# Gate and up products in the order wide, wide, narrow, narrow, and a planner with a larger margin and fewer weight pieces

## The chip, the core and the metric

The kernel runs on one core of one Trainium2 chip. The metric is the device time of one execution in microseconds (us). Three timed runs of the kernel before gave 1286.79, 1289.82 and 1290.23 us; the median is 1289.82. The profiled execution is one more run with times of its own. TensorE is called PE in the rows, VectorE DVE, ScalarE ACT, GpSimd POOL and SyncE, whose queue issues the transfers here, SP.

## The reference: what is computed

Two layers of a hybrid decoder trunk run over 256 positions of width 1024, all in float32:

```python
for l in range(DEPTH):                       # 2 layers, D_FF = 2816
    x = x + 0.5 * swiglu(rms_norm(x, ffn1_norm[l]), ffn1_w_gate_up[l], ffn1_w_down[l])
    u = rms_norm(x, mix_norm[l]) @ w_in[l]
    ...                                      # u is split: SSD, mLSTM and RWKV-7 mixers
    y = jnp.concatenate([y_ssd, y_ml, y_rw], axis=-1)
    x = x + y @ w_out[l]
    x = x + 0.5 * swiglu(rms_norm(x, ffn2_norm[l]), ffn2_w_gate_up[l], ffn2_w_down[l])
return rms_norm(x, final_norm)

def swiglu(x, w_gate_up, w_down):
    gate, up = jnp.split(x @ w_gate_up, 2, axis=-1)
    return (jax.nn.silu(gate) * up) @ w_down
```

So there are four feed-forward stages (two in each layer) with a mixer stage between the two of each layer. Each layer's weights are read once.

## The kernel before

**Split products.** TensorE multiplies in a reduced float32 format. To keep float32 accuracy each operand is split into a high part (ScalarE copies it into that format, L821 for weights) and a low part (VectorE subtracts, L822), and a product is hi x hi + hi x lo + lo x hi. `mm3` (L853 to L856) does this with three matmuls.

**A gate and up block.** A feed-forward stage has 22 blocks of 128 gate and 128 up columns. The first two are computed together in another form; the other 20 are done by `gate_up`. There the activations are the moving operand: `hT.both(kk)` is the high and the low part of one 128-row slice of the normalised input side by side, 512 columns, and `hT(kk)[0]` is the high part alone, 256 columns. For each slice kk (8 of them) and each of gate and up (g) there is a wide matmul (L1073, weights' high part against both, 512 columns into the whole bank) and a narrow one (L1075, weights' low part against the high part, 256 columns into the bank's second half). A block is 16 wide and 16 narrow matmuls, into two banks. The kernel before issues wide, narrow for gate, then wide, narrow for up; for the last slice the narrow one goes first, so that the wide one (L1078) closes the bank. Behind each block come the down products of the block two before it (`down`, 12 matmuls of 512 columns, by `mm3`).

**The mixers.** The input projection `w_in` is computed in blocks of 24 matmuls of 256 columns (`block`, by `mm3`) and in wide parts. Each block's result goes through a token shift (L1185) or three convolution steps on VectorE (L1195). Beside these dense products run three chains of small dependent work: the gates (VectorE lines L1557 to L1621 with transposes L1552, L1595, L1618 and sums L1582), mLSTM and SSD (the exponentials' rows by L1631 and L1632, mLSTM's first products L1653 with its weights wq, wk, wv read by L1647), and RWKV. The RWKV chain matters below: 32 small matmuls (L1299) are masked on VectorE (L1304, eight operations), parts of the result go to memory in 32 small transfers (L1338) and come back as one tile (L1341), thirty small VectorE steps solve a triangular system in it (L1364, L1366), the result goes through memory again (L1371, L1372, L1380), and TensorE continues with transposes that are told to wait for the solve (L1388, L1398) and with the block products of L1428 and L1474.

**What sets the order.** The program is recorded, and a planner (class `Planner`) then simulates the engines with its own costs and emits the instructions in the order in which it placed them. Each engine's queue, and the queue of transfers, keeps that order on the chip. For an instruction whose inputs come from another engine the planner lets TensorE count it as due only MARGIN ns after these inputs are ready, by its own clock; a dense product that is due earlier goes first (`est`). This delay is only in the choice: no wait is put into the program. `allowed` limits how many weight pieces are held: raw ones as they land ("f") and split ones ("r"), at least wmin, at most wmax and only while enough room is left. `keep` holds room back for the mixers' tiles; the values are tried in order until a plan succeeds, which it does at 4096.

Of the kernel before, what the change touches and what calls it, by code (L numbers as in the profile page):

```python
# [28 lines left out]
T = 256  # L29
# [128 lines left out]
class Planner:  # L158


    SEM = 60.0
    MARGIN = 1000.0
    SWITCH = 1283.0

    def __init__(self, nc, pool, banks, smalls):
# [194 lines left out]
    def run(self, reserve, wmin, wmax, urgent, keep_max, spare):  # L360
# [132 lines left out]
        def est(op):  # L493
# [7 lines left out]
            if op.eng == "pe" and op.cross > 0:  # L501
                t = max(t, op.cross + self.MARGIN)
            if op.lock:
# [124 lines left out]
def kernel(ctx: ExitStack, tc: tile.TileContext, x, pvec, prow, fnorm, w_gate,  # L628
# [28 lines left out]
    banks = [psum.tile([128, 512], F32, name=f"bank{i}") for i in range(8)]  # L657

    plan = Planner(nc, ctx.enter_context(tc.tile_pool(name="regions", bufs=1)), banks, smalls)
    pe, act, dve, gps, sp = (plan.engine(n) for n in ("pe", "act", "dve", "gps", "sp"))  # L660
# [347 lines left out]
    def ffn(inp, update, make_next, first=None):  # L1008
# [3 lines left out]
        hT = inp.hT  # L1012
# [47 lines left out]
        def gate_up(j, R):  # L1060


            banks = [mmb(), mmb()]
            for i in range(2):
                (w,) = weights(1)
                wh, wl = (v.rearrange("p (k g c) -> p k g c", k=4, g=2) for v in w[1:])
                with dense(w):
                    for k in range(4):
                        kk = 4 * i + k
                        for g in range(2):  # L1070
                            o = banks[g]
                            if kk < 7:
                                pe.matmul(o, lhsT=wh[:, k, g, :], rhs=hT.both(kk), start=kk == 0, stop=False,  # L1073
                                          skip_group_check=True)
                            pe.matmul(o[:, T:], lhsT=wl[:, k, g, :], rhs=hT(kk)[0], start=False, stop=False,  # L1075
                                      skip_group_check=True)
                            if kk == 7:
                                pe.matmul(o, lhsT=wh[:, k, g, :], rhs=hT.both(kk), start=False, stop=True,  # L1078
                                          skip_group_check=True)
            with ranked(1):  # L1080
                s, u = new(T), new(T)
                hi, lo = pt_pair(j, 1)
# [832 lines left out]
    for l in range(DEPTH):  # L1915
# [2 lines left out]
        inp, update = ffn(inp, update, lambda: ToFfn(pv[:, l + 1, C_N1:C_N1 + 8]) if l + 1 < DEPTH  # L1918
                          else ToOut(fnorm[0:D]))
    inp.tile(1, update)  # L1920
    assert any(plan.run(reserve={"f": 6144, "r": 6144}, wmin={"f": 4, "r": 4}, wmax={"f": 5, "r": 6},
                        urgent={"act": 7000.0, "dve": 5500.0}, keep_max=keep, spare=8)
               for keep in (3072, 4096, 6144, 8192)), plan.jam
    with tc.manual_schedule():
        plan.emit()
    return plan
# [58 lines left out]
```

## Time and profile before

| what | value |
|---|---|
| median of three runs | 1289.82 us |
| profiled execution, its own time | 1287.25 us |
| its span, first to last instruction | 1285.5 us |
| TensorE busy | 1248.3 us, 97% of the span |
| VectorE, ScalarE, GpSimd busy | 70%, 55%, 7% |
| read from memory | 207 MB, 162 GB/s over the span |

The stages by the time in the span: feed-forward to about 195 us, the first mixer to about 450, two feed-forward stages to about 830, the second mixer to about 1085, the last feed-forward stage. In a row of a table by stage stand the window, its length, busy time of PE, weight loads, DVE, ACT and POOL with their counts, then the granted TensorE clock, the DMA share and GB/s. A row in order of time has start, duration, engine, line, operation, output and input, size, count, and in brackets the idle time before it and what ended it. Matmuls overlap, so their pace is the distance of their starts. A row of waits has the total, the number and the longest, in us.

### The profile page before, as it was taken

What the parts mean: (1) busy time and instruction counts of PE and PEld (TensorE: products, weight loads), DVE (VectorE), ACT (ScalarE), POOL (GpSimd) and SP (SyncE); (2) the same over time, 40 slices, a digit from 0 to 9 for tenths busy, and PEclk for the clock granted to TensorE, in tenths of its full rate; (3) what the DMA queues carried; (4) which work ended last, traced back from release to release, by engine and by line L of the source; (5) the groups of instructions that cost most, each with busy time, mean ns of one, the idle gap of its engine ahead of it and who ended that gap; (6) DMA issues with size and microseconds to landing.
All of it is one profiled execution on the core that took longest, in us unless ns stands there. A gap on an engine that the chain in (4) does not pass through costs nothing.

```text
span 1285.5 us, 20959 instructions
## 1 busy us (share of the span) xinstructions
PE 1248.3 (97%) x7938; PEld 1074.8 (84%) x7938; DVE 897.2 (70%) x1448; ACT 713.0 (55%) x1237; POOL 86.3 (7%) x153
## 2 busy tenths in 40 slices
PE   8999999998999999999999999999899999999997
PEld 6888887987997888888888888789889888888886
DVE  7766666984798476666676666669837993766664
ACT  7555546665655365555565555565557553655553
POOL 3000002110100010000000000111100110000001
PEclk9999999999999999999999999999999999999999
DMA  9986663042168486665575764630513576757500
GB/s 304 362 279 187 184 179 83 1 131 42 52 198 278 147 287 206 196 196 145 164 215 169 218 186 135 164 97 3 141 33 116 177 260 202 214 180 210 167 1 33
DMA packets 281876, 210.22 MB, mean 164 GB/s; under 512 B 23856, under 2 KB 257200, under 8 KB 281776
## 3 DMA queue, kind: packets, MB, share of 16 engines
q1 hardware_dynamic: 281776, 208.89, 53.3%
q8 instruction: 62, 1.02, 0.3%
q14 instruction: 38, 0.31, 0.1%
HBM read 207.01 MB, written 1.84 MB: 162 GB/s over the span
## 4 chain that ended last, share of the span: by engine, by line
PE 85%; DVE 7%; ACT 4%; issue 1%; SPq 1%; DMA 1%; POOL 0%; POOLq 0%; DVEq 0%; ACTq 0%
PE bank L1073 20%; PE bank L855 13%; PE bank L854 13%; PE bank L856 13%; PE bank L1075 12%; PE bank L1078 3%; PE bank L1428 2%; DVE region L822 1%; PE bank L1805 1%; DVE region L1195 1%; ACT region L821 1%; PE bank L1492 1%; PE bank L1511 1%; ACT region L886 1%; PE bank L1662 1%
## 5 line engine op out<-in xcount | busy, mean ns | idle before, releaser
L822 DVE TENSOR_TENSOR region<-region,region 128x1024 fp32r<-128x1024 f32 (+1 forms) x382 | 444.3, 1208 | 52.7 <-ACT region L821 49.8
L1073 PE MATMUL bank<-region,region 128*128 128x512 f32 x1120 | 398.2, 398 | 0.0
L854 PE MATMUL bank<-region,region 128*128 128x512 f32 (+1 forms) x1104 | 387.6, 351 | 0.8 <-DVE region L1304 0.4
L856 PE MATMUL bank<-region,region 128*128 128x512 f32 (+1 forms) x1104 | 385.8, 350 | 0.3 <-DVE region L873 0.3
L855 PE MATMUL bank<-region,region 128*128 128x512 f32 (+1 forms) x1104 | 385.9, 350 | 0.0
L821 ACT ACTIVATE region<-region 128x1024 fp32r<-128x1024 f32 (+1 forms) x382 | 376.7, 1038 | 12.0 <-PE bank L855 4.8
L1075 PE MATMUL bank<-region,region 128*128 128x256 f32 x1280 | 346.5, 281 | 0.0
L1073 PEld LDWEIGHTS bank<-region,region 128*128 128x128 f32 x1120 | 210.4, 188 | 50.9
L1075 PEld LDWEIGHTS bank<-region,region 128*128 128x128 f32 x1280 | 241.6, 189 | 6.6
L855 PEld LDWEIGHTS bank<-region,region 128*128 128x128 f32 x1104 | 211.5, 192 | 27.9 <-issue 2.0
L856 PEld LDWEIGHTS bank<-region,region 128*128 128x128 f32 x1104 | 211.3, 191 | 27.7 <-issue 1.7
L854 PEld LDWEIGHTS bank<-region,region 128*128 128x128 f32 x1104 | 211.4, 191 | 25.9 <-DVE region L1304 0.8
L1086 ACT ACTIVATE region<-bank 128x256 f32<-128x256 f32 (+1 forms) x84 | 30.9, 373 | 220.1 <-PE bank L1078 220.1
L1088 DVE TENSOR_TENSOR region<-bank,region 128x256 f32<-128x256 f32 (+1 forms) x84 | 34.2, 411 | 126.8 <-ACT region L1086 126.8
L873 DVE TENSOR_TENSOR region<-region,region 128x256 fp32r<-128x256 f32 (+2 forms) x88 | 37.0, 425 | 35.6 <-ACT region L872 35.6
L1090 ACT ACTIVATE region<-region 128x256 f32<-128x256 f32 (+1 forms) x84 | 34.0, 408 | 49.2 <-DVE region L1089 49.2
L1078 PE MATMUL bank<-region,region 128*128 128x512 f32 x160 | 60.2, 399 | 0.0
L872 ACT ACTIVATE region<-region 128x256 fp32r<-128x256 f32 (+2 forms) x88 | 36.2, 416 | 37.6 <-DVE region L1092 37.3
L886 ACT ACTIVATE region<-res 128x512 f32<-128x512 f32 x28 | 17.6, 628 | 56.2 <-DVE res L882 53.8
L890 POOL TENSOR_SCALAR smalls<-smalls 128x1 f32<-128x1 f32 x14 | 6.7, 476 | 617.7 <-ACT region L886 617.5
L1195 DVE SCALAR_TENSOR_TENSOR region<-bank,pv,region 128x255 f32<-128x255 f32 (+2 forms) x84 | 39.9, 479 | 7.2 <-ACT region L1193 5.3
L1092 DVE TENSOR_TENSOR region<-region 128x256 f32<-128x256 f32 (+1 forms) x75 | 31.6, 422 | 11.4 <-ACT region L1090 4.2
(304 smaller groups left out, 1075.5 us busy)
## 6 DMA issues: line engine op xcount, KB each, us to landing
region<-in_f_gu_dram SPq DMA_DIRECT2D x352, 256.0 KB, 4.8
region<-in_f_dn_dram SPq DMA_DIRECT2D x88, 512.0 KB, 4.8
region<-in_w_in_dram SPq DMA_DIRECT2D x80, 512.0 KB, 4.5
region<-in_w_out_dram SPq DMA_DIRECT2D x32, 512.0 KB, 4.8
region<-in_prow_dram SPq DMA_DIRECT2D x4, 512.0 KB, 5.1
region<-in_prow_dram SPq DMA_DIRECT2D x6, 256.0 KB, 3.9
region<-in_w_gate_dram SPq DMA_DIRECT2D x2, 512.0 KB, 4.8
dn<-region SPq DMA_DIRECT2D x64, 4.0 KB, 1.4
```

What stands on the lines that cost most here:

```text
L821: act.activation(out=hi[:, c], in_=src[:, c], func=AF.Copy)
L822: dve.tensor_tensor(out=lo[:, c], in0=src[:, c], in1=hi[:, c].bitcast(F32), op=ALU.subtract)
L854: pe.matmul(o, lhsT=ah, rhs=bh, start=start, stop=False, skip_group_check=True)
L855: pe.matmul(o, lhsT=ah, rhs=bl, start=False, stop=False, skip_group_check=True)
L856: pe.matmul(o, lhsT=al, rhs=bh, start=False, stop=stop, skip_group_check=True)
L872: act.activation(out=hi, in_=src, func=AF.Copy)
L873: dve.tensor_tensor(out=lo, in0=src, in1=hi.bitcast(F32), op=ALU.subtract)
L1073: pe.matmul(o, lhsT=wh[:, k, g, :], rhs=hT.both(kk), start=kk == 0, stop=False, skip_group_check=True)
L1075: pe.matmul(o[:, T:], lhsT=wl[:, k, g, :], rhs=hT(kk)[0], start=False, stop=False, skip_group_check=True)
L1078: pe.matmul(o, lhsT=wh[:, k, g, :], rhs=hT.both(kk), start=False, stop=True, skip_group_check=True)
L1088: dve.tensor_tensor(out=s[:, ts], in0=gate[:, ts], in1=s[:, ts], op=ALU.add)
L1195: dve.scalar_tensor_tensor(out=dst[:, s:T], in0=ps[:, 0:T - s], scalar=col(cw + 3 - s), in1=dst[:, s:T], op0=ALU.mult, op1=ALU.add)
```

## The change

Three edits. `gate_up` issues, for each slice, the two wide products and then the two narrow ones; the last slice is treated like the others, so that a narrow product closes each bank. MARGIN goes from 1000 to 2000 ns. The planner may hold 4 raw and 5 split weight pieces in place of 5 and 6, and its list of `keep` values begins at 4096.

```diff
     SEM = 60.0
-    MARGIN = 1000.0
+    MARGIN = 2000.0
     SWITCH = 1283.0
...
                     for k in range(4):
-                        kk = 4 * i + k
                         for g in range(2):
-                            o = banks[g]
-                            if kk < 7:
-                                pe.matmul(o, lhsT=wh[:, k, g, :], rhs=hT.both(kk), start=kk == 0, stop=False,
-                                          skip_group_check=True)
-                            pe.matmul(o[:, T:], lhsT=wl[:, k, g, :], rhs=hT(kk)[0], start=False, stop=False,
-                                      skip_group_check=True)
-                            if kk == 7:
-                                pe.matmul(o, lhsT=wh[:, k, g, :], rhs=hT.both(kk), start=False, stop=True,
-                                          skip_group_check=True)
+                            pe.matmul(banks[g], lhsT=wh[:, k, g, :], rhs=hT.both(4 * i + k), start=i == k == 0,
+                                      stop=False, skip_group_check=True)
+                        for g in range(2):
+                            pe.matmul(banks[g][:, T:], lhsT=wl[:, k, g, :], rhs=hT(4 * i + k)[0], start=False,
+                                      stop=i == 1 and k == 3, skip_group_check=True)
...
-    assert any(plan.run(reserve={"f": 6144, "r": 6144}, wmin={"f": 4, "r": 4}, wmax={"f": 5, "r": 6},
+    assert any(plan.run(reserve={"f": 6144, "r": 6144}, wmin={"f": 4, "r": 4}, wmax={"f": 4, "r": 5},
                         urgent={"act": 7000.0, "dve": 5500.0}, keep_max=keep, spare=8)
-               for keep in (3072, 4096, 6144, 8192)), plan.jam
+               for keep in (4096, 6144, 8192)), plan.jam
```

Since five lines go, the lines below `gate_up` are five lower in the changed kernel (L1304 becomes L1299, L1338 becomes L1333, L1398 becomes L1393, L1653 becomes L1648), and the wide and narrow products are L1070 and L1073.

On TensorE, at the start of a gate and up block of the first feed-forward stage (bank4 and bank5 are gate and up; the regions are split weights and activations), before the change:

```order
L856 MATMUL bank2_89<-region4_276,region9_235 128x512
L1073 MATMUL bank4_91<-region2_129,region6_628 128x512
L1075 MATMUL bank4_91<-region2_129,region6_628 128x256
L1073 MATMUL bank5_92<-region2_129,region6_628 128x512
L1075 MATMUL bank5_92<-region2_129,region6_628 128x256
```

and after it, where bank2 and bank3 are gate and up:

```order
L856 MATMUL bank5_92<-region6_152,region10_239 128x512
L1070 MATMUL bank2_89<-region4_134,region7_366 128x512
L1070 MATMUL bank3_90<-region4_134,region7_366 128x512
L1073 MATMUL bank2_89<-region4_134,region7_366 128x256
L1073 MATMUL bank3_90<-region4_134,region7_366 128x256
```

The second wide product now follows a wide one, and the two narrow ones stand together.

On VectorE, in the first layer's mixer, around the eight masked products (region_2180 is the first half of the RWKV matrix; region_1040 holds the gates), before:

```order
L1289 TENSOR_TENSOR region_1841<-region_2120,region_911 128x1024
L822 TENSOR_TENSOR region_352<-region_584,region_352 128x1024
L822 TENSOR_TENSOR region_498<-region_1040,region_498 128x1024
L822 TENSOR_TENSOR region_1753<-region_584,region_1753 128x1024
L1304 TENSOR_TENSOR region_2180<-bank_88,maskar 128x4x128
...
L1304 TENSOR_TENSOR region_347<-bank_88,maskar 128x4x128
L1557 TENSOR_TENSOR region_1040<-bank_89,sgn 128x72
L1561 SCALAR_TENSOR_TENSOR region_1040<-region_1040 128x72
```

and after (region_2192 and region_298 are the matrix's halves, region_752 the gates):

```order
L1284 TENSOR_TENSOR region_1096<-region_2135,region_2035 128x1024
L1552 TENSOR_TENSOR region_752<-bank_87,sgn 128x72
...
L822 TENSOR_TENSOR region_134<-region_1096,region_134 128x1024
L1561 TENSOR_TENSOR region_752<-region_752 128x72
...
L1567 SCALAR_TENSOR_TENSOR region_752<-region_752 128x72
L1299 TENSOR_TENSOR region_2192<-bank_90,maskar 128x4x128
L1299 TENSOR_TENSOR region_2192<-bank_91,maskar 128x4x128
L1567 SCALAR_TENSOR_TENSOR region_752<-region_752 128x72 x3
L1299 TENSOR_TENSOR region_2192<-bank_92,maskar 128x4x128
...
L1567 SCALAR_TENSOR_TENSOR region_752<-region_752 128x72 x2
```

The gates' steps moved ahead of the masks, and six of the eight masks stand behind four of the gates' steps.

On the queue of transfers, behind the 32 small ones to `dn` of the same layer (weight blocks of `w_in` by L746), before:

```order
L1338 DMA dn<-region_347 16x4x16
L746 DMA region_2420<-in_w_in_dram 128x8x128 x2
L746 DMA region_781<-in_w_in_dram 128x8x128
L1647 DMA region_454<-in_wq_dram 128x4x128
L1341 DMA region_1040<-dn 128x256
L1647 DMA region_454<-in_wk_dram 128x4x128
L1647 DMA region_454<-in_wv_dram 128x4x128
```

and after:

```order
L1333 DMA dn<-region_298 16x4x16
L1642 DMA region_2431<-in_wq_dram 128x4x128
L1642 DMA region_2431<-in_wk_dram 128x4x128
L1642 DMA region_2431<-in_wv_dram 128x4x128
L746 DMA region_2453<-in_w_in_dram 128x8x128
L1336 DMA region_1954<-dn 128x256
```

The three weights of mLSTM come directly behind the small transfers, and a weight block stands ahead of the read back. Ahead of the first small transfer stood 92 pieces of weights, and now 89 do.

## The prediction

> **What bounds the kernel now.** I read the page's engine totals first, then busy time by stage, then TensorE's rows in order of time, and last who waits for whom in the mixers.
>
> ```profile
> span 1285.5 us, 20959 instructions
> PE 1248.3 (97%) x7938; PEld 1074.8 (84%) x7938; DVE 897.2 (70%) x1448; ACT 713.0 (55%) x1237; POOL 86.3 (7%) x153
> ...
> 500.00:550.00 50.00, 50.00 (x264) 42.73 (x264) 33.19 (x48) 26.22 (x43) 0.00 (x0) 1.00 0.62 189
> ...
> 245.00:295.00 50.00, 44.36 (x369) 42.12 (x368) 43.47 (x107) 26.60 (x59) 9.48 (x18) 0.95 0.33 91
> 295.00:345.00 50.00, 47.84 (x701) 43.84 (x699) 26.24 (x55) 31.07 (x70) 3.09 (x4) 0.98 0.14 28
> ...
> 830.00:880.00 50.00, 47.27 (x294) 41.29 (x293) 37.11 (x46) 30.73 (x49) 7.61 (x11) 0.93 0.30 83
> 880.00:930.00 50.00, 44.28 (x374) 41.31 (x372) 44.30 (x105) 28.64 (x63) 9.19 (x18) 0.99 0.32 90
> 930.00:980.00 50.00, 48.72 (x703) 44.88 (x702) 22.01 (x39) 31.13 (x67) 1.86 (x2) 0.98 0.17 35
> ```
>
> TensorE (PE) is the bound. In the feed-forward stages (500 to 550) it is never idle, so there only the matmuls' own pace counts. In the mixers it is idle for 5.6 of 50 us in the first layer's middle and 5.7 in the second's, and its granted clock falls: 1 minus the clock times the window gives 2.5 + 1.0 us in the first layer and 3.5 + 0.5 + 1.0 in the second, 8.5 us of lost pulses. These are two separate accounts, and the change touches each with a different part.
>
> **The order of gate and up products.** A busy figure for a pipelined matmul is not its pace, so I take start times.
>
> ```profile
> 110.05 0.28 PE L1075 MATMUL bank<-region,region 128*128 128x256 f32 x1
> ...
> 111.47 0.28 PE L1075 MATMUL bank<-region,region 128*128 128x256 f32 x1
> ...
> 111.81 0.40 PE L1075 MATMUL bank<-region,region 128*128 128x256 f32 x2
> 112.05 0.40 PE L1078 MATMUL bank<-region,region 128*128 128x512 f32 x1
> ...
> 112.87 0.40 PE L855 MATMUL bank<-region,region 128*128 128x512 f32 x1
> ...
> 115.37 0.39 PE L1073 MATMUL bank<-region,region 128*128 128x512 f32 x1
> ```
>
> From 110.05 to 111.47 lie four pairs of a wide (512 columns) and a narrow (256) product: 1.42 / 4 = 0.355 us each. From 112.87 to 115.37 lie eleven wide products behind one another (the down products): 2.50 / 11 = 0.227. The two narrow ones that already stand together take 112.05 - 111.81 = 0.24, or 0.12 each. So a pair costs 0.008 us more (0.355 against 0.227 + 0.120) than its parts cost next to their own kind: a wide product pays about 8 ns when a narrow one stood before it. Today 15 of a block's 16 wide products follow a narrow one. In the new order 7 do, and the block now ends narrow, so that the first down product becomes an eighth. Seven turns fewer x 8 ns x 80 blocks (20 in each of four feed-forward stages) = 4.5 us. Against it: a narrow product alone between two wide ones takes 0.11 to 0.12, so that the second narrow of a pair may cost up to 4 ns more; 7 more such pairs x 4 ns x 80 = 2.2 us. I take the middle, -3.3 us, between 0 (the pace depends on the sum of columns alone) and -4.5. No stage hides it, since TensorE has no idle time there. What the block leaves behind: the gate bank used to be complete one narrow and one wide product before the block's end and is now complete one narrow product before it, 0.23 us later. Its evacuation feeds a down product two blocks on, over 8 us later, so this costs nothing outside the last block of a stage.
>
> **Weights held.** The planner keeps one raw and one split piece less, and TensorE's weights are converted less far ahead. In the feed-forward stages the conversions have room: VectorE (DVE) is busy 33 of 50 us. I cost this at 0; what hides it is the pieces still held, and if that cover were gone a piece would be late by the conversion (the L822 row below), about 1.2 us each time. The list of reserves without 3072 changes nothing: the plan is made with 4096 in both kernels.
>
> **The margin.** It delays TensorE's dependent matmuls by 1 us against the planner's own clock and lets dense products stand in front of them. It can win only where TensorE now waits:
>
> ```profile
> PE bank L1398 <- DVE region L1621: 2.4, 1, 2.4
> ...
> PE bank L1428 <- issue: 1.0, 2, 0.5
> ...
> PE bank L1582 <- DVE region L1578: 1.0, 1, 1.0
> PE bank L1299 <- DVE region L1304: 0.9, 1, 0.9
> PE bank L1474 <- ACT region L1399: 0.9, 1, 0.9
> PE bank L1631 <- DVE region L1366: 0.6, 1, 0.6
> ...
> PE bank L1398 <- DVE region L1195: 2.3, 1, 2.3
> ...
> PE bank L1582 <- DVE region L1185: 1.4, 1, 1.4
> ...
> PE bank L1428 <- issue: 0.9, 1, 0.9
> ...
> PE bank L922 <- ACT region L926: 0.7, 2, 0.3
> ```
>
> The first six rows are layer 0's (the L1299 wait is in both layers), the next three layer 1's, the last one the start of a feed-forward stage. Without L1299, which waits for a bank and not for the margin, layer 0 has 5.9 us and layer 1 has 4.6. The three later feed-forward starts may lose a third of 0.7 each: -0.7 us.
>
> In the mixers the new order does not only push matmuls back; it also changes what the RWKV chain waits for on VectorE and on the DMA queue (SP).
>
> ```profile
> 256.28 4.87 DVE L1304 TENSOR_TENSOR region<-bank,maskar 128x512 f32<-128x512 f32 x8
> ...
> 258.19 15.85 SPq L1338 DMA_DIRECT2D dn<-region  x32
> ...
> 277.91 0.58 SPq L1341 DMA_DIRECT2D region<-dn  x1
> ...
> 279.01 0.51 SPq L1647 DMA_DIRECT2D region<-in_wv_dram  x1
> ...
> 291.34 0.17 DVE L1366 TENSOR_TENSOR region<-region 128x15 f32<-128x15 f32 x1
> ...
> 293.56 0.98 PE L1398 MATMUL bank<-ident,region 128*128 128x128 f32 x4 [2.37 <-DVE region L1621]
> ...
> region<-in_wv_dram SPq DMA_DIRECT2D x2, 256.0 KB, 4.5
> ...
> L822 DVE TENSOR_TENSOR region<-region,region 128x1024 fp32r<-128x1024 f32 (+1 forms) x382 | 444.3, 1208 | 52.7 <-ACT region L821 49.8
> ...
> L1195 DVE SCALAR_TENSOR_TENSOR region<-bank,pv,region 128x255 f32<-128x255 f32 (+2 forms) x84 | 39.9, 479 | 7.2 <-ACT region L1193 5.3
> ```
>
> The chain: eight mask products (L1304) end at 261.1; the queue writes them out with 32 issues in 15.85 us; the read back (L1341) is at 277.9; thirty small VectorE steps (L1364, L1366) end at 291.5; then the transposes of L1398 may start, which now wait 2.4 us. In the new VectorE order the gate chain comes ahead of the masks and the last six masks stand behind four of its L1572 steps. That puts the masks about 3.5 us later (two conversions of 1.21 leave their front; the small gate steps, one conversion and the gates' detour over ScalarE come in), and with them the 32 issues, wq, wk, wv and every weight piece behind. Inside the thirty steps there now stand three conversions and six L1195 operations, where three L1195 stood: 3 x 1.21 + 3 x 0.48 = 5.0 us more. The steps started some 1.4 us after their data could be there (277.9 + 0.6 + some 3 us) because of a conversion and a triple ahead of them, which are gone: in sum 3.5 + 5.0 - 1.4 = 7.1, an estimate, so the solve ends at 298.6.
>
> TensorE, meanwhile, has 35 more narrow products ahead of L1398 (35 x 0.12 = 4.2 us), six more pairs of L1631 and L1632, and one more of L1653. By the rows below a pair takes 2 x 0.12.
>
> ```profile
> 284.63 0.28 PE L1631 MATMUL bank<-br,selr 128*128 128x256 f32 x1
> ...
> 284.98 0.28 PE L1632 MATMUL bank<-maskr,identr 128*128 128x256 f32 x1
> ```
>
> That is 4.2 + 1.4 + 0.2 = 5.8 us. It would have come to L1398 at 293.56 - 2.37 = 291.2, so now at 297.0. On the way it meets a new wait: ten pairs, which now begin near 281, stand ahead of the first L1653 products, so these are due at about 282 to 283, and wv, third behind the 32 issues, lands near 258.2 + 3.5 + 15.9 + 2 + 4.5 = 284.1: I take 2 us. The waits of L1631 (0.6) and its neighbour go. So it reaches L1398 at 297 to 298.5 and waits 0 to 1.6 more; I take 1.5, because the steps' own start is the loosest number. What is late next: the second pair of DMA trips (L1371 to L1380) starts 7 us later, but 65 more dense products stand in front of L1428, so the L1474 and L1428 waits should go. Layer 0: 1.0 (L1582) + 2 + 1.5 = 4.5 against 5.9, -1.4; layer 1, with the same order, 4.5 against 4.6, -0.1. Bounds: all of these waits gone, -10.5; the two waits at 4 and 5 us in each layer, 1.0 + 9 = 10 against 5.9 and 4.6, +9.5. The value is near the middle, since chain and cover move back by nearly the same.
>
> **Sum.** -3.3 - 0.7 - 1.5 = -5.5. The profiled execution took 1287.25 us (span 1285.5), 2.6 below the median of 1289.82; I make the sum against the former, 1281.8, and put the same distance back on for the median: 1284.3.
>
> On the order, the Trainium skill (TensorE: Matmul & The Clock Gate, section Back-to-back issue gap) gives columns / 2.4 + 2.5 ns for a matmul behind another, which does not depend on the neighbour. By it the order would be worth 0; the 0.355 against 0.347 above speaks against it, by little.
>
> **Rivals.** *The margin takes nearly all the waits* (18%): the dense products last longer than the chain is late. For it: TensorE gets 5.8 us more cover. Against: the chain moves by 7.1. Eight of the 10.5 us go, and lost pulses with them: the five windows above are idle for 17.5 us and lose 8.5, so 0.49 us for each idle one (in the forecast's 1.5 this is left out, as too little to end a low stretch). 1289.8 - 3.3 - 0.7 - 8 x 1.49 = 1273.9.
>
> *The order is worth nothing* (21%): columns alone set the pace, and 0.355 is something else, such as the change of bank. The rest stays: 1289.8 - 2.2 = 1287.6.
>
> *Slower* (17%): the queue behind the 32 issues decides. One queue holds the masks' writes, wv and the weight pieces of the next blocks; three pieces fewer stand ahead of it (89 against 92), and TensorE needs piece 89 now only 38 narrow products (4.6 us) after the first L1653. If the masks are over 5 us late, wv lands after 286 and the solve ends after 301: waits of 4 and 5 us in each layer, +9.5, with the pulses x 1.49: 1289.8 - 4.0 + 14.2 = 1300. Against it: the queue stands still for 44 us today, and no weight is late.
>
> ```profile
> SPq L1338 <- DVE region L1304: 44.3, 2, 44.0
> ```
>
> On that price, the Trainium skill (TensorE: Matmul & The Clock Gate, section What's actually happening) lets the clock fall to half after an idle window of about 3.4 us; this trace loses pulses in windows whose longest single wait is 2.4, so the waits need not be that long.
>
> **How the numbers follow.** Forecast 44%, its own range 1280 to 1289. For this kernel 0.3% is 3.9 us, about what a measurement can tell from no change: below 1285.9 is faster, above 1293.7 slower. Faster: 0.6 of the forecast, nearly all of the first rival, little of the second: 0.47. Slower: four fifths of the last rival and a little of the forecast's tail: 0.16. The rest, 0.37, is no change. Range: from just above the first rival's time to between the forecast and the last one's, 1275 to 1295.
>
> **What would show it.** Right: a new block of gate and up products takes about 40 ns less, first wide to first down product; wide products behind wide ones start 0.227 apart. In the mixers: the masks end near 264.5, the solve near 298, a wait for DMA at the products of wv (L1648 in the new numbering), none at L1423. Wrong: a feed-forward stage of the same length (then the order is worth nothing), idle time at weights in any feed-forward stage, TensorE idle over 15 us in a mixer, or no wait at all at L1393.

## The result, and the profile after

The changed kernel takes 1281.65 us (median; 1280.69 to 1283.2), the kernel before 1288.3 beside it. The ratio is 0.9949, 95% interval 0.9938 to 0.9961: 6.6 us less. The forecast was 1284.3 in a range of 1275 to 1295. The profiled execution took 1280.8 us, against the 1281.8 of the sum. The page's totals and the windows by stage:

```profile
span 1279.1 us, 21014 instructions
...
PE 1236.7 (97%) x7938; PEld 1067.8 (83%) x7938; DVE 894.2 (70%) x1448; ACT 700.3 (55%) x1233; POOL 91.7 (7%) x153
...
245.00:295.00 50.00, 42.45 (x365) 39.80 (x363) 38.93 (x96) 27.62 (x64) 8.51 (x18) 1.00 0.35 96
295.00:345.00 50.00, 49.18 (x681) 44.50 (x680) 27.77 (x55) 31.32 (x69) 0.00 (x0) 1.00 0.36 92
...
880.00:930.00 50.00, 43.90 (x369) 41.68 (x368) 40.18 (x101) 25.75 (x61) 8.45 (x17) 0.97 0.35 96
930.00:980.00 50.00, 47.99 (x676) 43.76 (x675) 27.61 (x50) 32.06 (x70) 0.00 (x0) 1.00 0.39 99
```

TensorE's busy time fell by 11.6 us (1248.3 to 1236.7), its idle time rose from 37.2 to 42.4. In the first layer's middle it is idle for 7.6 of 50 us where it was 5.6, but the granted clock is 1.00 there instead of 0.95. So the change made TensorE's work shorter and its waits longer.

One block of gate and up products, before and after, by TensorE's rows in order of time:

```profile
502.56 0.39 PE L1073 MATMUL bank<-region,region 128*128 128x512 f32 x1
...
508.20 0.39 PE L854 MATMUL bank<-region,region 128*128 128x512 f32 x1
```

```profile
501.37 0.62 PE L1070 MATMUL bank<-region,region 128*128 128x512 f32 x2
501.82 0.40 PE L1073 MATMUL bank<-region,region 128*128 128x256 f32 x2
502.05 0.63 PE L1070 MATMUL bank<-region,region 128*128 128x512 f32 x2
502.52 0.39 PE L1073 MATMUL bank<-region,region 128*128 128x256 f32 x2
...
506.93 0.40 PE L854 MATMUL bank<-region,region 128*128 128x512 f32 x1
```

From the first wide product to the first down product lie 508.20 - 502.56 = 5.64 us before, and 506.93 - 501.37 = 5.56 after. Over all blocks that no other work interrupts the means are 5.642 (76 blocks) and 5.563 (72), and none lies over 3 ns from its mean. 80 blocks x 0.078 = 6.3 us.

I split the profiled executions into stretches, each from the start of its first gate and up product to the start of the product behind its last one. What lies between two stretches counts as a mixer, with the norms around it. The feed-forward stretches together took 680.8 us before and 674.4 after (-6.4); the two mixers 566.1 and 563.7 (-2.4); the start 21.6 and 23.1 (+1.5), and the work behind the last feed-forward stage +0.9. That is -6.4 in all.

The waits of TensorE after, and the RWKV chain of layer 0 in order of time:

```profile
PE bank L922 <- DMA res<-in_x_dram: 4.0, 1, 4.0
...
PE bank L854 <- DVE region L1190: 3.2, 3, 2.4
...
PE bank L1648 <- ACT region L1630: 3.0, 1, 3.0
...
PE bank L854 <- DVE region L1359: 2.1, 1, 2.1
...
PE bank L1648 <- DMA region<-in_wv_dram: 1.9, 1, 1.9
...
PE bank L1423 <- DVE region L1436: 0.6, 1, 0.6
```

```profile
260.76 3.67 DVE L1299 TENSOR_TENSOR region<-bank,maskar 128x512 f32<-128x512 f32 x6
...
261.48 16.37 SPq L1333 DMA_DIRECT2D dn<-region  x32
...
280.23 1.01 SPq L1336 DMA_DIRECT2D region<-dn  x1
...
283.16 0.65 PE L1648 MATMUL bank<-region,region 128*128 128x128 f32 x4
...
285.16 1.06 ACT L821 ACTIVATE region<-region 128x1024 fp32r<-128x1024 f32 x1 [3.52 <-DMA region<-in_w_in_dram]
...
285.50 0.19 DVE L1359 TENSOR_TENSOR region<-region 128x15 f32<-128x15 f32 x1 [4.67 <-DMA region<-dn]
...
286.12 1.64 ACT L1630 ACTIVATE region<-bank,region 128x128 f32<-128x128 f32 x6
...
286.78 0.71 PE L1648 MATMUL bank<-region,region 128*128 128x128 f32 x4 [2.97 <-ACT region L1630]
...
292.47 1.51 DVE L1190 SCALAR_TENSOR_TENSOR region<-bank,pv,region 128x255 f32<-128x255 f32 x3
...
294.13 0.36 PE L854 MATMUL bank<-region,region 128*128 128x256 f32 x1 [2.08 <-DVE region L1359]
...
298.43 0.17 DVE L1361 TENSOR_TENSOR region<-region 128x15 f32<-128x15 f32 x1
```

The wait before L854 is a new kind: a dense product of the input projection needs a bank, and what empties the bank is a triple of L1190 operations that the plan has put in the middle of the solve's steps. The row names a step of the solve as the releaser. But the triple ends at 292.47 + 1.51 = 293.98, and the product's weight load starts at 294.10, before that step has ended (294.11).

The wait of 2.97 us before L1648 is of the same kind. The weight wv landed at 283.04 us, and the first four products that need it ran at 283.16. The next four need a bank that ScalarE empties by L1630. L1630 stood behind a conversion (L821) for whose weight ScalarE waited 3.52 us. That weight is the block of `w_in` that the queue holds behind the 32 small transfers and the three weights of mLSTM. In layer 1 the wait of 1.86 us is for wv itself: it landed at 914.14, and its products began at 914.27.

### The profile page after: what moved, and what is told of

Same layout as the page of the kernel before. It is cut to its first block, busy times and chain, and to the rows that moved or that the text cites. A ratio compares the mean times of both kernels' runs of the same rounds, so it can differ in the third digit from the quotient of the medians.

```text
span 1279.1 us, 21014 instructions
## 1 busy us (share of the span) xinstructions
PE 1236.7 (97%) x7938; PEld 1067.8 (83%) x7938; DVE 894.2 (70%) x1448; ACT 700.3 (55%) x1233; POOL 91.7 (7%) x153
## 5 line engine op out<-in xcount | busy, mean ns | idle before, releaser
L1070 PE MATMUL bank<-region,region 128*128 128x512 f32 x1280 | 402.1, 395 | 0.0
L821 ACT ACTIVATE region<-region 128x1024 fp32r<-128x1024 f32 (+1 forms) x382 | 377.9, 1039 | 30.1 <-DMA region<-in_w_in_dram 7.8
L854 PE MATMUL bank<-region,region 128*128 128x512 f32 (+1 forms) x1104 | 385.9, 350 | 6.4 <-DVE region L1190 3.2
L856 PE MATMUL bank<-region,region 128*128 128x512 f32 (+1 forms) x1104 | 383.7, 349 | 3.4 <-DVE region L873 2.9
L1073 PEld LDWEIGHTS bank<-region,region 128*128 128x128 f32 x1280 | 240.2, 188 | 55.3
L1073 PE MATMUL bank<-region,region 128*128 128x256 f32 x1280 | 252.9, 278 | 0.0
L854 PEld LDWEIGHTS bank<-region,region 128*128 128x128 f32 x1104 | 209.9, 190 | 31.5 <-DVE region L1190 2.6
L856 PEld LDWEIGHTS bank<-region,region 128*128 128x128 f32 x1104 | 209.7, 190 | 30.6 <-DVE region L873 3.8
L855 PEld LDWEIGHTS bank<-region,region 128*128 128x128 f32 x1104 | 210.0, 190 | 23.4 <-issue 1.7
L1070 PEld LDWEIGHTS bank<-region,region 128*128 128x128 f32 x1280 | 200.9, 189 | 6.6 <-DVE region L873 0.3
L1190 DVE SCALAR_TENSOR_TENSOR region<-bank,pv,region 128x255 f32<-128x255 f32 (+2 forms) x84 | 39.9, 479 | 4.7 <-ACT region L1187 2.6
L872 ACT ACTIVATE region<-bank 128x512 fp32r<-128x512 f32 x28 | 16.6, 599 | 41.3 <-PE bank L1202 20.3
L1087 DVE TENSOR_TENSOR region<-region 128x256 f32<-128x256 f32 (+1 forms) x70 | 28.7, 413 | 9.7 <-ACT region L1085 2.6
```

The costliest lines, as they stand in the source:

```text
L821: act.activation(out=hi[:, c], in_=src[:, c], func=AF.Copy)
L854: pe.matmul(o, lhsT=ah, rhs=bh, start=start, stop=False, skip_group_check=True)
L855: pe.matmul(o, lhsT=ah, rhs=bl, start=False, stop=False, skip_group_check=True)
L856: pe.matmul(o, lhsT=al, rhs=bh, start=False, stop=stop, skip_group_check=True)
L872: act.activation(out=hi, in_=src, func=AF.Copy)
L1070: pe.matmul(banks[g], lhsT=wh[:, k, g, :], rhs=hT.both(4 * i + k), start=i == k == 0, stop=False, skip_group_check=True)
```

## Experiments

My theory after the result: the order of the products alone carries the gain, and the planner edits are about neutral. Two rivals: they carry half of it through fewer stretches at half clock (five in the run before, one after), or they cost time that the order pays for. A summary first; "margin" is 2000 in place of 1000, "pieces" one raw and one split piece less, "reserve" the `keep` with which the plan succeeded. "Feed-forward" and "mixers" are the sums in one profiled execution, as above, which can lie up to 4 us from the median (that without the margin took 1284.05, that without the order 1287.42). "Idle" is TensorE's idle time in the two mixers, and "half clock" half of the time that they spent at a granted clock of 0.5.

| kernel | reserve | median, us | ratio to before (95%) | block, us | feed-forward | mixers | idle | half clock |
|---|---|---|---|---|---|---|---|---|
| before | 4096 | 1288.3 | 1 | 5.642 | 680.8 | 566.1 | 22.5 | 8.5 |
| after | 4096 | 1281.65 | 0.9949 (0.9938 to 0.9961) | 5.563 | 674.4 | 563.7 | 25.0 | 1.7 |
| order | 4096 | 1280.87 | 0.9944 (0.9931 to 0.9958) | 5.563 | 674.9 | 564.1 | 22.6 | 3.4 |
| margin, pieces | 3072 | 1292.29 | 1.0028 (1.0016 to 1.0041) | 5.642 | 679.1 | 571.4 | 24.7 | 11.9 |
| margin | 6144 | 1294.78 | 1.0052 (1.0038 to 1.0067) | 5.642 | 679.7 | 574.5 | 30.2 | 11.9 |
| pieces | 3072 | 1284.72 | 0.9975 (0.9966 to 0.9985) | 5.642 | 680.7 | 562.9 | 21.0 | 3.4 |
| after without the order | 4096 | 1290.18 | 1.0012 (1.0002 to 1.0021) | 5.642 | 679.0 | 566.5 | 22.5 | 8.5 |
| after without the margin | 4096 | 1280.33 | 0.9948 (0.9932 to 0.9964) | 5.565 | 674.4 | 568.4 | 24.1 | 8.5 |
| after without the pieces | 4096 | 1284.03 | 0.9966 (0.9956 to 0.9977) | 5.563 | 674.3 | 568.4 | 24.2 | 10.2 |
| after with the old list | 3072 | 1287.88 | 1.0007 (0.9995 to 1.0018) | 5.563 | 674.4 | 568.4 | 27.1 | 5.1 |
| after, strict turns, other bank | 4096 | 1295.32 (one run) | | 5.638 | 679.9 | 573.0 | 27.1 | 11.9 |
| after, eight and eight | 4096 | 1285.57 (one run) | | 5.559 | 675.3 | 567.5 | 31.0 | 0.0 |
| after, merged writes | 4096 | 1277.48 | 0.9925 (0.9908 to 0.9942) | 5.563 | 674.4 | 560.2 | 22.8 | 3.4 |
| merged writes, margin 1000 | 4096 | 1286.85 | 0.9985 (0.9972 to 0.9998) | 5.565 | 674.4 | 574.1 | 28.2 | 10.2 |

The mixers less their idle time and less the half clock come to 532 to 539 us in all fourteen. So what differs between them is how long TensorE waits (21 to 31 us) and how much clock it loses (0 to 12 us). The second differs from run to run of one kernel too: before took 1284.9 to 1290.2 us over 23 runs, the shorter the higher the clock (see the last section). So one profiled sum of the mixers should not be read more finely than some 5 us.

The table has another pattern. In the seven kernels with both the margin of 2000 and fewer pieces, ScalarE waits 3.1 to 5.2 us in the mixers for one late weight of `w_in`, in both layers (with merged writes only in the first). In the other seven it waits at most 0.3 us for such a weight. In all of the first seven but the merged one, TensorE then stands 2.6 to 3.1 us in the first layer, before the product that is L1648 in the changed kernel.

**The order alone.** Before, with only the loops of `gate_up` changed as in the diff.

> Only the new order of the gate and up products; margin, pieces held and list of reserves as before. The changed kernel is 6.6 us faster, and its 80 blocks of gate and up products take 5.563 us each instead of 5.642. Theory 'order': the block alone carries the gain, so the blocks here take 5.563 too and the kernel is faster by 80 x 0.078 = 6.3 us (about 1282), with the mixers as long as before (282 and 284 us). Theory 'half': the two planner edits give part, through fewer half-clock stretches in the mixers (five before, one in the changed kernel, 1.7 us each at most): the gain here is only 3 to 4 us (about 1285) although the blocks are short. Theory 'cost': the planner edits lose time in the mixers (their idle time grew by 2.4 us), so that this kernel is faster than the changed one, by 8 us or more against before (1280).

1280.87 us, 0.9944. The blocks are as short as in the changed kernel, and so is the time. "Half" (1285) falls. "Cost" wanted a gain of 8 us or more; the interval is 5.4 to 8.9 us, so this run does not exclude it. The three planner edits together are worth nothing that can be told beside the new order.

**The planner edits with the old order.** First together, then one by one:

```diff
-    MARGIN = 1000.0
+    MARGIN = 2000.0
...
-... wmax={"f": 5, "r": 6},
+... wmax={"f": 4, "r": 5},
```

> Only the two planner edits (margin 2000, one raw and one split weight piece less); products in the old order. Blocks should take 5.642 us as before. Theory 'order': same time as before within 1 us. Theory 'half': faster by 3 us, mixers shorter, and at most two half-clock stretches. Theory 'cost': slower by 2 us or more, TensorE idle in the mixers 2 us longer than before. My recorded terms for the same edits were -0.7 and -1.5, so -2.2 us.

> Only the margin of 2000; pieces held as before, products in the old order. By the recorded steps (weights held: 0) it should be as the kernel with both planner edits, -2.2 us, with the waits at the products of wv, at the two transposes of the solve and at the gates moved as in the changed kernel. If the pieces matter, it differs from that kernel by over 1 us.

> Only one raw and one split weight piece less; margin 1000 and products in the old order. Recorded step: 0, so the time of before within 1 us, no wait for a weight in any feed-forward stage, the mixers' waits in the places of before. If the pieces carry part of the gain (conversions stand less far ahead of the chains on VectorE), the masks and the solve end earlier than before (261.1 and 291.5 us) and the mixers are shorter by 1 us or more.

+0.28%, +0.52% and -0.25%: none is neutral. The blocks are at 5.642 in all three, so the difference lies elsewhere, most of it in the mixers (+5.3, +8.4 and -3.2 us in the profiled runs). With the margin alone the longest wait is this one in the first layer (VectorE's and TensorE's rows of that kernel, numbered as before):

```profile
287.00 0.18 DVE L1364 TENSOR_TENSOR region<-region 128x15 f32<-128x15 f32 x1 [4.34 <-DMA region<-dn]
...
294.06 0.17 DVE L1366 TENSOR_TENSOR region<-region 128x15 f32<-128x15 f32 x1
...
294.56 1.51 DVE L1195 SCALAR_TENSOR_TENSOR region<-bank,pv,region 128x255 f32<-128x255 f32 x3
...
296.22 0.55 PE L1631 MATMUL bank<-br,selr 128*128 128x256 f32 x1 [6.71 <-DVE region L1195]
```

VectorE first waits 4.34 us for the read back, then does the thirty steps, and only then the triple that empties a bank. TensorE needs that bank and stands for 6.71 us. It is the wait of the changed kernel at 294.13 in a worse place. It is not the whole loss: TensorE's idle time rises by 3.7 us in the first layer and by 4.0 in the second, where a wait of 3.40 us at L1428 is the longest, and 3.4 us more go by half clock.

These three plans were not made with one reserve (see the table: with the margin alone none can be made with 4096, and with fewer pieces 3072 succeeds). So they do not price one edit each, and I undid the parts one at a time from the other end, where 4096 stays.

**Undoing the order, the margin, the pieces, the list.**

```diff
-... for keep in (4096, 6144, 8192)), plan.jam
+... for keep in (3072, 4096, 6144, 8192)), plan.jam
```

That is the last of the four; the others put back the old loops, MARGIN = 1000, and wmax 5 and 6.

> The whole change but for the order of the products: margin 2000, one raw and one split piece less, no reserve of 3072, old order. The kernels so far were planned with different reserves (4096 for before, after and the order alone; 3072 for margin with pieces and for pieces alone; 6144 for the margin alone, which cannot be planned with 4096), so their planner effects are not one edit each. This one is planned with 4096 as before and after are. If the parts add up and the order is worth 80 x 0.078 = 6.3 us, it takes 1281.7 + 6.3 = 1288.0, the time of before, with blocks of 5.642 us and mixers as in the changed kernel (281.9 and 281.7 us). If every edit of the products also reshuffles the mixers, their sum can be some 3 to 8 us longer, as with margin and pieces (571 us against 566), and it takes 1291 to 1295.

> The change with the old margin of 1000 (new order, one raw and one split piece less, reserve 4096). If the parts add up, -7.8 for the order alone and -4.0 for the pieces alone: about 1277, with at most two half-clock stretches and mixers under 281 us each. If the sum of the mixers is settled by each plan anew, 563 to 567 us as in before, after and the order alone, it takes 1279 to 1284 and can not be told from the changed kernel.

> The change with the old number of pieces (new order, margin 2000, reserve 4096). If a margin of 2000 costs what it cost alone (+6.1 us, by a wait of 6.7 us for a bank whose evacuation stands behind the thirty steps of the solve on VectorE), this takes 1281 + 6 = 1287. If that wait came from the one plan, this takes 1280 to 1283 like the changed kernel, and no wait for a bank is over 3.5 us.

> The changed kernel with 3072 put back at the front of the list of reserves. In before a plan with 3072 can not be made, so that the list changed nothing there; with one piece less of each kind it can, and then it is what is used. Recorded step: the list is worth nothing, 1281.7. If every new plan moves the mixers, their sum (563.7 in the changed kernel) differs by 2 to 5 us either way with the blocks at 5.563: 1278 to 1286.

Without the order: 1290.18, so the order is worth some 8 us beside the other edits (1.0012 against 0.9949) and some 7 alone (0.9944), of which 6.3 are the blocks. Without the margin: 1280.33, not to be told from the changed kernel; the 1277 of adding up the parts did not come. Without the pieces: 1284.03, 2.4 more, though the two intervals of the ratio touch, with a wait for a bank like the one above:

```profile
926.90 0.55 PE L854 MATMUL bank<-region,region 128*128 128x256 f32 x1 [5.09 <-DVE region L1190]
```

That lies between the two times that were expected, and the wait is over the 3.5 us of the better case. At a margin of 1000 the pieces make no difference beside the new order (1280.87 with all of them, 1280.33 with fewer). With the old list: 1287.88, which is 6.2 more, as much as the whole gain and outside both expectations. Its blocks and feed-forward stretches are those of the changed kernel; its mixers are longer by 4.7 and its start by 1.5. Beside the wait at L1648 that the changed kernel has too, the profile shows one that it puts down to a weight of the input projection, for which TensorE did not wait in the changed kernel's mixers:

```profile
PE bank L1648 <- ACT region L1630: 2.6, 1, 2.6
PE bank L1423 <- DMA region<-in_w_in_dram: 2.4, 1, 2.4
```

**What of the order costs.** In the old order each narrow product writes the bank that the wide one ahead of it wrote; in the new one no two neighbours share a bank. That is another reason than the turns, and it can be separated:

```diff
 for k in range(4):                           # strict turns, other bank
-    w0(k); w1(k); n0(k); n1(k)
+    w0(k); n1(k)
+for k in range(4):
+    w1(k); n0(k)
```

(w0 is the wide product into bank 0, n1 the narrow one into bank 1; in the first slice of a block both wide products come first. In two places of a block, where one loop follows another, two neighbours still share a bank; before there were 16.) The other kernel takes all eight wide products of a weight piece, then its eight narrow ones.

> The changed kernel with wide and narrow products in strict turns again, but so that each goes into the other bank than the one ahead of it: per weight piece w0 n1 four times, then w1 n0 four times (the first slice of a block takes both its wide ones first). Before, turns were strict and each narrow product went into the bank of the wide one ahead of it: 5.642 us a block; the changed kernel has pairs and no two neighbours in one bank: 5.563. If the turn between wide and narrow is what costs, a block takes 5.63 to 5.65 here too. If writing the same bank twice running is what costs, it takes 5.56 to 5.57.

> The changed kernel with all eight wide products of a weight piece first and then its eight narrow ones: two changes from narrow to wide in a block in place of eight, no two neighbours in one bank, as in the changed kernel. If each turn costs, a block comes to 16 x (0.227 + 0.120) = 5.552 us or up to 5 ns above (at most 0.9 us in the whole kernel). If the bank is what costs, it stays at 5.563.

TensorE's rows, of the first kernel and of the second:

```profile
505.68 0.62 PE L1069 MATMUL bank<-region,region 128*128 128x512 f32 x2
506.13 0.28 PE L1073 MATMUL bank<-region,region 128*128 128x256 f32 x1
506.24 0.40 PE L1069 MATMUL bank<-region,region 128*128 128x512 f32 x1
...
511.31 0.40 PE L854 MATMUL bank<-region,region 128*128 128x512 f32 x1
```

```profile
504.70 1.98 PE L1069 MATMUL bank<-region,region 128*128 128x512 f32 x8
506.51 1.11 PE L1073 MATMUL bank<-region,region 128*128 128x256 f32 x8
507.46 2.00 PE L1069 MATMUL bank<-region,region 128*128 128x512 f32 x8
509.30 1.12 PE L1073 MATMUL bank<-region,region 128*128 128x256 f32 x8
510.25 0.40 PE L854 MATMUL bank<-region,region 128*128 128x512 f32 x1
```

Strict turns into the other bank: 511.31 - 505.68 = 5.63 (mean 5.638). The bank explains 4 ns of the 78, the turns the rest. But a turn has no fixed price either: from 14 of the 16 narrow products standing alone to pairs a block loses 78 ns, from pairs to groups of eight (two changes from narrow to wide in place of eight) only 4 more. And those 4 do not last: behind a block of eights the twelve down products take 2.747 us, behind one of pairs 2.730. Block and down products together take 8.307 us with eights and 8.293 with pairs, and the feed-forward stretches 675.3 and 674.4. So what costs most is a single narrow product between two wide ones, and pairs are the best of the four orders. Why, the trace does not show. The second kernel is slower than the changed one by some 4 us in its one run, most of it in the mixers (567.5 against 563.7).

**A shorter chain.** In the chain of layer 0 above the 32 transfers of L1333 hold the queue for 16.37 us. I merged them in pairs to 16 of twice the size, by another order of the axes in the tile:

```diff
-NMv = [new(2048).rearrange("p (n c h t) -> p n c h t", ...
+NMv = [new(2048).rearrange("p (c n h t) -> p n c h t", ...
...
-for h in range(2):
-    for i in range(2):
-        sp.dma_start(out=dnv[c, b16][:, i * 4:i * 4 + 4, h, :],
-                     in_=NMv[i][rows_of(c, b16), :, c, h, c0:c0 + 16])
+for i in range(2):
+    sp.dma_start(out=dnv[c, b16][:, i * 4:i * 4 + 4].rearrange("s n h t -> s (n h) t"),
+                 in_=NMv[i][rows_of(c, b16), :, c, :, c0:c0 + 16].rearrange("p n h t -> p (n h) t"))
```

> The changed kernel with the 32 small transfers that write out the masked products merged in pairs to 16 (both heads of a pair in one transfer, the same bytes). They take 16.3 us of the one queue (261.5 to 277.8), and the read back, the weights of the mLSTM and the thirty steps of the solve stand behind them. If an issue costs the same 0.5 us whatever it moves, the writes take 8 us, the solve starts and ends 6 to 8 us earlier (near 291 in place of 298.6), the waits at the products of wv (3.0 and 1.9 us) go, and the two mixers together are 3 to 6 us shorter: 1276 to 1279. If an issue costs by the rows that it moves, nothing changes in the chain (16 us). If the new plan only trades one wait for another, the mixers' sum stays within 563 to 569 us and the time within 1280 to 1287.

1277.48 us, the lowest median of all: 0.9925 of before, with an interval that just touches that of the changed kernel. Part of the queue's and VectorE's rows:

```profile
262.34 8.87 SPq L1332 DMA_DIRECT2D dn<-region  x16
...
281.27 0.18 DVE L1358 TENSOR_TENSOR region<-region 128x15 f32<-128x15 f32 x1
...
292.02 0.17 DVE L1360 TENSOR_TENSOR region<-region,region 128x15 f32<-128x15 f32 x1
```

The solve ended 6.4 us earlier (292.0 against 298.4 for the start of its last step), as the issue theory has it. But the first layer's mixer, whose solve this is, took 282.5 us against 281.9 in the profiled runs; the second took 277.7 against 281.7. So I tried the same in the other good plan, with the margin at 1000.

> The merged writes once more, in another plan: new order, one piece of each kind less, margin 1000. Without the merge this took 1280.3 (1278.5 to 1284.1) with mixers of 283.6 and 284.8 us. If the shorter chain (16 issues in 8.9 us in place of 32 in 16.3, as measured with the margin of 2000) is what gained 4 us there, it gains 3 to 5 us here as well: 1275 to 1277, with the solve over 6 us earlier than 291.3. If that gain was the lot of one plan, this one falls anywhere between 1278 and 1287.

There it loses some 5 us (0.9985 of before against 0.9948 without the merge; medians 1286.85 and 1280.33):

```profile
261.25 7.97 SPq L1332 DMA_DIRECT2D dn<-region  x16
...
274.97 0.18 DVE L1358 TENSOR_TENSOR region<-region 128x15 f32<-128x15 f32 x1
...
281.95 1.51 DVE L1190 SCALAR_TENSOR_TENSOR region<-bank,pv,region 128x255 f32<-128x255 f32 x3
...
283.58 0.17 DVE L1360 TENSOR_TENSOR region<-region,region 128x15 f32<-128x15 f32 x1
...
283.61 0.35 PE L854 MATMUL bank<-region,region 128*128 128x256 f32 x1 [2.26 <-DVE region L1358]
```

The chain is shorter here too: the solve is done at 283.8, 7.5 us before that of the kernel without the merge (291.3). TensorE waits all the same, 2.26 us for a bank whose triple again stands among the steps, and there is another such wait in the second layer (2.36). Its idle time in the mixers is 4.1 us longer than without the merge. So the theory that the length of this chain sets the mixers has fallen. The gain of the merged kernel with the margin of 2000 is a measured gain of that one plan; I can not say that merging is what brought it. Part of what sets the mixers is where each plan puts the work that empties a bank: among the solve's steps, or behind a late weight. Which waits make up the idle time of each of the fourteen plans stays open.

## Why the prediction was right, and where it was not

**Order of the products: -3.3 predicted, -6.3 measured, beyond the bound of -4.5.** Direction and place were right: the gain lies in the stages without idle time and comes with fewer turns. The failing step is the fixed price of a turn. The forecast took 8 ns for each wide product behind a narrow one, removed seven of the fifteen, let eight keep their price, and gave back up to 4 ns for the second narrow product of a pair. Over whole blocks the old order lay 90 ns above 16 x 0.347 = 5.552 us, 6 ns for each of its 15 turns. The new one lies 11 ns above it and still has seven turns and an eighth behind it. So the turns that were left did not keep their price, and 79 of the 90 ns went. The pairs took nothing back: from start to next start, the 16 narrow products of a block became 30 ns shorter together and the 16 wide ones 49. The reading behind the price was coarse too: the 0.355 for a pair, from four pairs at two decimals, is 0.3526 over whole blocks, and a wide product behind a wide one is 0.232 from it and not the 0.227 that I named as a sign.

On the same step, the Trainium skill (TensorE: Matmul & The Clock Gate, section Back-to-back issue gap) gives the isolated gap of a matmul by its columns alone. By that formula the four orders measured here, with the same products, would take the same time. They took 5.642, 5.638, 5.563 and 5.559 us a block.

**Weights held: 0 predicted.** Right for the feed-forward stages: with the new order they take 674.3 to 674.9 us with either number of pieces. In the mixers the pieces that are left were not cover enough: beside the margin of 2000, ScalarE waited 3.52 and 4.26 us for a weight in the two layers, and the first of these waits became TensorE's longest there. The step had looked at the feed-forward stages alone. For the whole kernel undoing it costs 2.4 us at this margin, at the edge of what can be told, and nothing at the old one.

**The list of reserves: "changes nothing" was wrong.** True is that both kernels are planned with 4096. But with fewer pieces 3072 succeeds, and that plan is 6.2 us slower. With the old order the same difference is 2 us (1292.29 against 1290.18). The edit does nothing alone; beside the other it changes the plan.

**Feed-forward starts: -0.7 predicted, -0.7 measured.** The waits of L922 for L926 at the three later starts sum to 2.1 us before and 0.9 after, where a new wait of 0.5 at L856 stands beside them. It goes with the margin: over the fourteen kernels the waits at L922 sum to 1.7 to 2.1 us with 1000 and to 0.35 to 1.05 with 2000. Two of the three starts lie in what the table counts as mixers. What the step left out is the first start and the end. The start takes 21.6 to 22.8 us with 1000 and 22.6 to 24.7 with 2000, the work behind the last feed-forward stretch 17.1 to 17.4 and 17.7 to 18.1; why was not looked into.

**Mixers: -1.5 predicted, -2.4 measured, by another way.** On VectorE and the queue the chain was predicted well: masks to 264.5 (264.4), 32 issues in some 16 us (16.37), end of the solve 298.6 (298.6). For TensorE it was not. A wait at wv came in the second layer (1.86 us for the 2); in the first the products of wv began 0.1 us after it had landed, and the 2.97 us that stand at the same line are for a bank, so the agreement there is luck. The wait at L1393 was put at 1.5 and did not come, which the prediction had named as a sign of being wrong; 2.1 and 2.4 us came before the dense products, for the banks behind the triples. I had counted these triples only as 0.48 each on the solve's way, not as something that TensorE waits for. TensorE's idle time in the mixers rose by 0.8 us in the first layer and 1.7 in the second, where -1.4 and -0.1 stood. What made up for it are pulses: 8.5 us of them were lost before and 1.7 after, a term that the forecast had left out "as too little" and that differs from run to run (see below). The late weight and the wait behind it are there only with the margin of 2000 and fewer pieces together; without the margin they are gone, but the kernel takes the same time.

**Rivals.** "The margin takes nearly all waits" is refuted by TensorE's idle time. "Slower" had its point of decision met by margin and pieces with the old order: there the masks ended 7.6 us later than before (268.7), wv landed at 287.5 and the solve ended at 303.2. The price did not come: the time was +0.28%, with longest waits of 2.9 and 2.2 us in that layer. With the margin alone it was +0.52%, and there neither wv (285.1) nor the end of the solve (294.2) was late. "The order is worth nothing" falls by the blocks. The sum, -5.5, came near the -6.4 of the profiled runs by luck: the order brought 3.0 us more than forecast, and 2.4 were lost at the start and the end, where the forecast had nothing.

## What to carry to other kernels

Price a reordering in a stage without idle time by the distance of starts over whole blocks, not over a few rows at two decimals, include what follows the block, and do not let short products stand alone between long ones: pairs did best here, and groups of eight gave their further gain back behind the block. Where a planner writes the order, each edit is also a new plan: here the mixers' sum went from 560 to 575 us over fourteen plans while the feed-forward stages told each edit's own price to 1 or 2 us, so judge the edit in the stage that the planner leaves alone, and count the plan as a draw that has to be measured. Up to 12 us of one execution's mixers were lost clock, so judge a plan by several runs. On an engine that keeps its order, look for work that empties another engine's buffers and stands behind a long dependent chain or a late weight, and ask whether a wait at the forecast line has the forecast cause.

## What the runs showed of the hardware

**Stretches at half clock lie on a fixed grid, and need no whole idle window.** All five within the run before last 3.41 us, and their distances are multiples of that (a sixth begins in the last 6 us). In other runs some last for two such windows. Windows of before on this grid (length, PE, weight loads, DVE, ACT, POOL, clock, DMA share, GB/s), and of after:

```profile
266.44:269.85 3.41, 2.18 (x17) 1.78 (x16) 3.13 (x11) 0.54 (x3) 0.62 (x3) 1.00 0.09 9
269.85:273.26 3.41, 3.41 (x19) 3.41 (x18) 3.41 (x6) 2.09 (x3) 2.29 (x4) 0.50 0.11 14
...
290.34:293.75 3.41, 1.04 (x10) 0.85 (x9) 2.89 (x13) 1.11 (x3) 0.00 (x0) 1.00 0.22 77
293.75:297.16 3.41, 3.41 (x18) 3.41 (x18) 0.69 (x1) 1.80 (x4) 0.00 (x0) 0.50 0.30 28
```

```profile
282.20:285.60 3.40, 1.61 (x14) 1.42 (x12) 0.10 (x1) 0.44 (x1) 0.00 (x0) 1.00 1.08 314
285.60:289.00 3.40, 2.22 (x18) 2.22 (x19) 3.09 (x12) 3.36 (x9) 0.00 (x0) 1.00 1.14 341
```

In before the clock halves for one window behind windows in which TensorE was busy for 2.18 and 1.04 us. In after a wait of 2.97 us falls across two windows, and nothing halves. The Trainium skill (TensorE: Matmul & The Clock Gate, section What's actually happening) tells of a free-running window of 3.4 us; the grid agrees. It lowers the clock after an idle window; here partly idle ones did. On the grids of the fourteen profiled runs, behind their first 8 us, every window at full clock with TensorE busy for less than 1.6 us was followed by one at half clock, and none with over 2.41. Between the two both occur (1.61 did not do it here, 2.18 did), so the busy time alone does not settle it. Where the grid falls differs from run to run, and the time with it: over 23 runs of before, at mean clocks of 0.990 to 0.998, the time falls from 1290.2 to 1284.9 us, with a correlation of -0.87.

**An issue costs by the transfer, not by its bytes.** In the rows of L1333 and L1332, 32 transfers of 4 KB took 16.37 us of the queue, 16 of 8 KB 7.97 and 8.87: 0.50 to 0.55 each.
